# First layer of a two-block network: gated linear attention with values and gates projected 512 columns wide

## The chip, the cores and the metric

One core of one Trainium2 chip runs the whole program; the other cores are idle. The metric is the device time of one execution in microseconds (us). TensorE is called PE here, VectorE DVE, ScalarE ACT, GpSimd POOL and SyncE SP.

## What is computed

The network has a first block of four layers (gated linear attention, spatial gating, forgetting attention, gated linear attention) and a second block of two layers with a context stream. The sequence is 512 tokens of width 1024. The change touches the mixer of layer 0 alone. Cut to what matters:

```python
GLA_HEADS, GLA_DK, GLA_DV = 4, 128, 256

def gla_mixer(h, w_in, w_a2, b_a, g_head, w_out):
    q, k, v, z, a_low = jnp.split(h @ w_in, [512, 1024, 2048, 3072], axis=-1)
    log_a = jax.nn.log_sigmoid(a_low @ w_a2 + b_a) / 16.0
    q = q * 128 ** -0.5
    # per head, chunk by chunk, with a running sum b of log_a inside a chunk:
    #   o     = (q * exp(b)) @ state + (causal, decayed q k^T) @ v
    #   state = exp(b_last) * state + (k * exp(b_last - b))^T @ v
    o = rms_norm(o, g_head)                 # per head
    return (o * jax.nn.silu(z)) @ w_out
```

The mixer is called for layers 0 and 3 with other weights.

## The kernel before

Every projection is made in three products, so that it keeps the precision of 32 bits: each operand is split into a high and a low part (`split`, L256: ACT writes the high part at L258, DVE or POOL the low part at L259), and PE adds high times high, high times low and low times high in one PSUM bank. The hidden state H is kept transposed and split, 8 pieces of 128 channels.

`proj_tok` (L290) makes a projection with the tokens on the partitions: a piece of H for one tile of 128 tokens is the stationary operand, the weights are streamed (L312, L313, L314). At 256 columns it loads two channel pieces of weights at a time (256 KB) and puts two token tiles in one PSUM bank, so that four tiles take two banks; it has four steps. At more than 256 columns each token tile has a bank of its own, weights come one channel piece at a time (256 KB again), and the last two pieces form one step: seven steps. `proj_T` (L344) makes queries and keys transposed, 512 tokens wide (L360 to L362), in two banks. The banks of projections are a ring of four (`pp`), those of all else another ring of four (`pa`).

`gla` (L663) runs head by head. Short names for its steps, with the head as a number:

- V: 256 columns of values (`values`, L670), two copies by ACT into SBUF (L675)
- decay: gates of the decay for all heads (`gla_decay`, L702), once
- Q: queries and keys of the head (L684), evicted by ACT (L686) and DVE (L687)
- P: the decayed products of queries and keys (`gla_pairs`, L738). Seven levels; each has two subtractions and a multiplication on DVE (L754, L755, L759), an exponential on ACT (L756), a multiplication on POOL (L758), four small products on PE (L765) and a masked copy on DVE (L769)
- Z: 256 columns of gates (L693), each bank evicted by ACT (L632) and then DVE (L633), multiplied by the head gain on POOL (L698)
- Hd: the scan over four chunks (`gla_head`, L772), which ends with transposes (L820); `Odone` (L654) then splits the head's output

The order in the program is V0, decay, Q0, P0, Z0, Hd0, and for each later head Q, P, V, Z, Hd. The output projection `outproj` follows, in four blocks of 256 columns; a block's four weight pieces belong to one head each, so three quarters of a block can run before the last head is done.

The generators hand control back at each `yield`. `drain` (L458) then does 0.6 of a step of a background queue in layer 0: modulation matrices for later layers are loaded (512 KB a step) and multiplied (`mods`, L382, products at L395). The order of the instructions on an engine is made when the program is built: a scheduler with a model of times takes the instruction of highest priority (earliest in the program) that its model has ready. On the chip each engine then runs its list in order.

Of the kernel before, what the change touches and what calls it, by code (L numbers as in the profile page):

```python
# [15 lines left out]
AF = mybir.ActivationFunctionType  # L16
ALU = mybir.AluOpType
# [59 lines left out]
class Core:  # L77
# [585 lines left out]
    def gla(self, H, j, O):  # L663
        nc, A = self.nc, self.A
        W = A["gla_w_in"][j]
        gh = self.bcast(A["gla_g_head"][j].rearrange("h d -> (h d)"), 1024, "t4")
        nc.vector.tensor_scalar(gh, gh, 0.5, None, ALU.mult)
        b = []

        def values(h, v):  # L670
            o = []
            yield from self.proj_tok(H, 4, W, 8, 1024 + h * 256, 256, o, lead=LEAD[0] if h == 0 else 1)
            v.append(self.t("t4", [128, 4, 256]))
            for i in range(2):
                nc.scalar.copy(v[0][:, 2 * i:2 * i + 2], o[0][i])  # L675

        for h in range(4):
            v = []
            if h == 0:

                yield from values(h, v)
                yield from self.gla_decay(H, j, b)
            o = []
            yield from self.proj_T(H, 512, W, 8, [h * 128, 512 + h * 128], o)  # L684
            qT, kT = self.t("t2", [128, 512]), self.t("t2", [128, 512])
            nc.scalar.activation(qT, o[0][0], AF.Copy, scale=128 ** -0.5)  # L686
            nc.vector.tensor_copy(kT, o[0][1])  # L687
            at = []
            yield from self.phase("glah", self.gla_pairs(b[h], qT, kT, at))
            if h:  # L690
                yield from values(h, v)
            o = []
            yield from self.proj_tok(H, 4, W, 8, 2048 + h * 256, 256, o)  # L693
            zg = self.t("t4", [128, 4, 256])
            for i in range(2):
                self.silu2(zg[:, 2 * i:2 * i + 2], o[0][i])
            for t in range(4):
                nc.gpsimd.tensor_tensor(zg[:, t], zg[:, t], gh[:, h * 256:(h + 1) * 256], op=ALU.mult)  # L698
            yield from self.phase("glah", self.gla_head(h, b[h], qT, kT, v[0], zg, at[0], O))
            self.Odone(O, h)  # L700

    def gla_decay(self, H, j, b):  # L702
# [69 lines left out]
    def gla_head(self, h, b, qT, kT, v, zg, at, O):  # L772
        nc = self.nc
        v4 = lambda x: x.rearrange("p (c n) -> p c n", c=4)
        eq = self.t("t2", [128, 512])
        nc.scalar.activation(eq, b, AF.Exp, scale=1.0 / 16)
        dec = self.small("gdec", [128, 4])
        nc.vector.tensor_copy(dec, v4(eq)[:, :, 127])
        qd = self.t("t2", [128, 512])
        nc.gpsimd.tensor_tensor(qd, qT, eq, op=ALU.mult)  # L780
        ek = self.t("t2", [128, 512])
        nc.vector.tensor_tensor(v4(ek), v4(b)[:, :, 127:128].to_broadcast([128, 4, 128]), v4(b), op=ALU.subtract)
        nc.scalar.activation(ek, ek, AF.Exp, scale=1.0 / 16)
        nc.vector.tensor_tensor(ek, kT, ek, op=ALU.mult)
        ps = self.psA()
        for c in range(3):
            cs = slice(c * 128, (c + 1) * 128)
            nc.tensor.transpose(ps[:, cs], ek[:, cs], self.ident)
        kd = self.t("t2", [128, 384])
        nc.scalar.copy(kd, ps[:, :384])  # L790
        yield
        ops = []
        S = None
        pos = []
        for c in range(4):
            cs = slice(c * 128, (c + 1) * 128)
            po = self.psA()
            nc.tensor.matmul(po[:, :256], at[:, c], v[:, c], start=True, stop=(c == 0))
            if c:
                nc.tensor.matmul(po[:, :256], qd[:, cs], S, start=False, stop=True)  # L800
            if c < 3:
                ps = self.psA()
                nc.tensor.matmul(ps[:, :256], kd[:, cs], v[:, c], start=True, stop=True)
                S2 = self.t("t1", [128, 256])
                if S is None:
                    nc.vector.tensor_copy(S2, ps[:, :256])
                else:
                    nc.vector.scalar_tensor_tensor(S2, S, dec[:, c:c + 1], ps[:, :256], ALU.mult, ALU.add)
                S = S2
            sq = self.t("t1", [128, 256])  # L810
            ss = self.small("ss", [128, 1])
            nc.scalar.activation(sq, po[:, :256], AF.Square, accum_out=ss)
            r = self.rstd1(ss, 256)
            if c % 2 == 0:
                ops.append(self.t("t2", [128, 2, 256]))
            nc.vector.scalar_tensor_tensor(ops[c // 2][:, c % 2], po[:, :256], r, zg[:, c], ALU.mult, ALU.mult)
        for kk in range(2):
            ps = self.psA()
            for c in range(4):
                nc.tensor.transpose(ps[:, c * 128:(c + 1) * 128], ops[c // 2][:, c % 2, kk * 128:(kk + 1) * 128],  # L820
                                    self.ident)
            nc.scalar.copy(self.Opiece(O, h * 2 + kk), ps)
        yield
# [1449 lines left out]
LEAD = (1, 1, 1, 1, 2)  # L2273
# [66 lines left out]
```

## Time and profile before

| | |
|---|---|
| median of 3 runs | 3252.29 us (3252.24 to 3263.88) |
| profiled execution | 3250.65 us |
| its span, first to last instruction | 3248.6 us |
| PE busy | 3074.4 us, 95% of the span |
| DVE, ACT, POOL busy | 1733.8, 1461.0, 1318.9 us |
| mean granted PE clock | 0.975 of 2.4 GHz |

The profile names instructions by line, engine, operation and tiles: `gla.pp` is a PSUM bank of a projection in the mixer, `glah.pa` one of P or Hd, `mods.pa` one of the background products, `out.pp` one of the output projection. "Idle before, releaser" is the time for which the engine stood still ahead of an instruction, and what ended it. A matmul's own duration overlaps its neighbours; from one start to the next is what it costs in a stream.

### The profile page before, as it was taken

The page shows a single profiled execution, that of the slowest core. Times are in us where ns is not written, and L with a number is a line of the kernel's source. Part 1 is how long each engine was busy: PE and PEld are TensorE (multiplying, and loading weights), DVE is VectorE, ACT ScalarE, POOL GpSimd, SP SyncE. Part 2 cuts the span into 40 slices and gives each one's busy share as a digit, 9 for nine tenths or more (in the row PEclk, how much of TensorE's full clock was granted, in tenths as well). Part 3 has the DMA queues.
Part 4 walks back from the last instruction along what each step waited for, and adds up shares of the span by engine and source line. Part 5 has one row for each costly group of instructions (what it writes and reads, how often), then busy time and mean ns, then how long its engine had stood idle before and what let it go on. Part 6 is the DMA issues. An engine that isn't in the chain of part 4 may idle for free.

```text
span 3248.6 us, 60794 instructions
## 1 busy us (share of the span) xinstructions
PE 3074.4 (95%) x23263; PEld 2642.0 (81%) x23263; DVE 1733.8 (53%) x3586; ACT 1461.0 (45%) x3205; POOL 1318.9 (41%) x1314
## 2 busy tenths in 40 slices
PE   7999999999999999998989999899999989999999
PEld 4878889878877788887877889898888967888887
DVE  2744564454555465666888667541444468641212
ACT  3434544454544543455545544443324357643323
POOL 2544453232212345454542123554555441254445
PEclk8999999999989999999999999899999989999999
DMA  7355645754435624234664334443555330043332
GB/s 240 92 153 171 214 133 164 228 172 127 134 118 177 180 61 103 61 114 124 178 176 119 104 103 131 145 130 114 167 190 163 103 82 2 29 141 98 97 123 90
DMA packets 477386, 426.20 MB, mean 131 GB/s; under 512 B 108022, under 2 KB 421577, under 8 KB 477097
## 3 DMA queue, kind: packets, MB, share of 16 engines
q1 hardware_dynamic: 477097, 422.33, 43.4%
q8 instruction: 183, 3.00, 0.4%
q14 instruction: 106, 0.87, 0.1%
HBM read 383.66 MB, written 38.01 MB: 130 GB/s over the span
## 4 chain that ended last, share of the span: by engine, by line
PE 41%; DVE 5%; POOL 2%; ACT 1%; issue 1%; DMA 1%; SPq 0%; POOLq 0%; DVEq 0%; ACTq 0%
PE ffn.pp L360 6%; PE ffn.pp L361 6%; PE ffn.pp L362 5%; PE ffn.pa L314 2%; PE ffn.pa L312 2%; PE ffn.pa L313 2%; PE odda.pa L1122 1%; PE odda.pa L931 1%; PE mla.pp L1745 1%; PE out.pp L312 1%; PE out.pp L314 1%; PE out.pp L313 1%; PE mla.pa L1122 1%; PE gdng.pa L1593 1%; PE ffn.pp L313 1%
## 5 line engine op out<-in xcount | busy, mean ns | idle before, releaser
L259 POOL TENSOR_TENSOR ffn.wl<-ffn.wr,ffn.wh 128x512 fp32r<-128x512 f32 x258 | 341.3, 1326 | 340.2 <-ACT ffn.wh L258 340.0
L258 ACT ACTIVATE ffn.wh<-ffn.wr 128x512 fp32r<-128x512 f32 x258 | 162.5, 631 | 342.4 <-PE ffn.pp L362 128.9
L360 PE MATMUL ffn.pp<-pre.t,ffn.wh 128*128 128x512 f32 x672 | 261.8, 390 | 0.0
L361 PE MATMUL ffn.pp<-pre.t,ffn.wl 128*128 128x512 f32 x672 | 261.5, 389 | 0.0
L362 PE MATMUL ffn.pp<-pre.t,ffn.wh 128*128 128x512 f32 x672 | 261.5, 389 | 0.0
L312 PE MATMUL gla.pp<-gla.wh,pre.t 128*128 128x256 f32 x512 | 151.5, 296 | 0.6 <-ACT pre.t L258 0.6
L313 PE MATMUL gla.pp<-gla.wl,pre.t 128*128 128x256 f32 x512 | 150.1, 293 | 0.0
L314 PE MATMUL gla.pp<-gla.wh,pre.t 128*128 128x256 f32 x512 | 149.1, 292 | 0.5 <-DVE pre.t L259 0.5
L259 POOL TENSOR_TENSOR gla.wl<-gla.wr,gla.wh 128x512 fp32r<-128x512 f32 x66 | 88.2, 1337 | 150.0 <-ACT gla.wh L258 141.2
L259 POOL TENSOR_TENSOR ffn.cwl<-ffn.cwr,ffn.cwh 128x512 fp32r<-128x512 f32 x44 | 61.3, 1392 | 214.4 <-ACT ffn.cwh L258 172.0
L360 PEld LDWEIGHTS ffn.pp<-pre.t,ffn.wh 128*128 128x128 f32 x672 | 126.2, 188 | 26.7 <-issue 0.8
L362 PEld LDWEIGHTS ffn.pp<-pre.t,ffn.wh 128*128 128x128 f32 x672 | 126.2, 188 | 26.3
L361 PEld LDWEIGHTS ffn.pp<-pre.t,ffn.wl 128*128 128x128 f32 x672 | 126.2, 188 | 26.1
L633 DVE SCALAR_TENSOR_TENSOR ffn.t<-ffn.t,ffn.pp 128x512 f32<-128x512 f32 (+1 forms) x66 | 39.3, 595 | 196.3 <-ACT ffn.t L632 196.2
L258 ACT ACTIVATE ffn.cwh<-ffn.cwr 128x512 fp32r<-128x512 f32 x132 | 82.9, 632 | 104.8 <-PE ffn.pp L362 40.6
L312 PE MATMUL sgu.pp<-sgu.wh,pre.t 128*128 128x256 f32 x384 | 112.0, 292 | 6.9 <-DVE gdnp.at L1306 6.0
L313 PE MATMUL ffn.pa<-ffn.wl,ffn.t 128*128 128x512 f32 x304 | 118.3, 389 | 0.0
L314 PE MATMUL ffn.pa<-ffn.wh,ffn.t 128*128 128x512 f32 x304 | 118.3, 389 | 0.0
L1177 DVE SCALAR_TENSOR_TENSOR ffn.t<-ffn.t,ffn.pp 128x512 f32<-128x512 f32 (+1 forms) x66 | 39.4, 597 | 143.6 <-PE ffn.pp L362 143.0
L395 PE MATMUL mods.pa<-mods.wm,cond_c 128*32 128x256 f32 x1152 | 100.4, 400 | 14.8 <-DMA mods.wm<-in_w_mod_dram 14.5
L312 PE MATMUL ffn.pa<-ffn.wh,ffn.t 128*128 128x512 f32 x304 | 112.7, 389 | 0.0
L312 PE MATMUL fox.pp<-fox.wh,pre.t 128*128 128x256 f32 x384 | 110.9, 289 | 0.7 <-ACT fox.t L1002 0.5
(831 smaller groups left out, 10757.0 us busy)
## 6 DMA issues: line engine op xcount, KB each, us to landing
mods.wm<-in_w_mod_dram SPq DMA_DIRECT2D x176, 512.0 KB
gla.wr<-in_gla_w_in_dram SPq DMA_DIRECT2D x96, 256.0 KB
ffn.wr<-in_w_ffn_gate_dram SPq DMA_DIRECT2D x88, 256.0 KB
ffn.wr<-in_w_ffn_up_dram SPq DMA_DIRECT2D x88, 256.0 KB
ffn.wr<-in_w_ffn_down_dram SPq DMA_DIRECT2D x88, 256.0 KB
fox.wr<-in_fox_w_in_dram SPq DMA_DIRECT2D x64, 256.0 KB
sgu.wr<-in_sgu_w_in_dram SPq DMA_DIRECT2D x48, 256.0 KB
out.res_x<-out.t SPq DMA_DIRECT2D x24, 512.0 KB
```

What stands on the lines that cost most here:

```text
L258: nc.scalar.activation(hi, src, AF.Copy)
L259: (lo_eng or nc.vector).tensor_tensor(lo, src, hi.bitcast(F32), op=ALU.subtract)
L312: nc.tensor.matmul(o, H.hi(kk, s), w[0][:, k], start=(kk == 0 and first), stop=False)
L313: nc.tensor.matmul(o, H.hi(kk, s), w[1][:, k], start=False, stop=False)
L314: nc.tensor.matmul(o, H.lo(kk, s), w[0][:, k], start=False, stop=(kk == K - 1 and last))
L360: nc.tensor.matmul(o, wh[:, k], H.hi(kk), start=(kk == 0), stop=False)
L361: nc.tensor.matmul(o, wl[:, k], H.hi(kk), start=False, stop=False)
L362: nc.tensor.matmul(o, wh[:, k], H.lo(kk), start=False, stop=(kk == K - 1))
L395: nc.tensor.matmul(ps[g * 32:(g + 1) * 32, :256], pad[:, j, :], ws[j][:, g * 256:(g + 1) * 256], start=(j == 0), stop=(j == 7))
L633: nc.vector.scalar_tensor_tensor(dst, dst, 1.0, z, ALU.add, ALU.mult)
L1122: nc.tensor.matmul(po[e * 64:(e + 1) * 64, it * 128:(it + 1) * 128], v(e, j), PT[e][:, j * 128:(j + 1) * 128], start=(j == 0), stop=(j == ...
L1177: nc.vector.scalar_tensor_tensor(f, sg, 0.5, o[1], ALU.mult, ALU.mult)
```

## The change

In layer 0 the values of heads 0 and 1 are projected together, 512 columns wide, ahead of head 0, and those of heads 2 and 3 together between P and Hd of head 1. The gates of heads 0 and 1 are projected together between P and Hd of head 0; the gates of heads 2 and 3 keep their own 256-wide projection. The order becomes V01, decay, Q0, P0, Z01, Hd0, Q1, P1, V23, Hd1, Q2, P2, Z2, Hd2, Q3, P3, Z3, Hd3. Layer 3 (`j` is 1) keeps the order of before in a copy of the old code. `gla_head` takes lists of chunks in place of tiles.

```diff
+        if j:
+            ...  (the loop of before, for layer 3)
+            return
+        def pieces(x, e, w=256):
+            return [x[t // 2][:, t % 2, e * w:(e + 1) * w] for t in range(4)]
+
         def values(h, v):
+            x = [self.t("t4", [128, 2, 512]) for _ in range(2)]
             o = []
-            yield from self.proj_tok(H, 4, W, 8, 1024 + h * 256, 256, o, lead=LEAD[0] if h == 0 else 1)
-            v.append(self.t("t4", [128, 4, 256]))
-            for i in range(2):
-                nc.scalar.copy(v[0][:, 2 * i:2 * i + 2], o[0][i])
+            yield from self.proj_tok(H, 4, W, 8, 1024 + h * 256, 512, o, lead=LEAD[0] if h == 0 else 1,
+                                     each=lambda t: nc.scalar.copy(x[t // 2][:, t % 2], o[0][t]))
+            v += [pieces(x, e) for e in range(2)]
+
+        def gates(h, n, z):
+            x = [self.t("t4", [128, 2, n * 256]) for _ in range(2)] if n > 1 else [self.t("t4", [128, 4, 256])]
+            o = []
+            if n > 1:
+                def each(t):
+                    self.silu2(x[t // 2][:, t % 2], o[0][t])
+                    nc.gpsimd.tensor_tensor(x[t // 2][:, t % 2], x[t // 2][:, t % 2], gh[:, h * 256:(h + n) * 256], op=ALU.mult)
+                yield from self.proj_tok(H, 4, W, 8, 2048 + h * 256, 512, o, each=each)
+                z += [pieces(x, e) for e in range(n)]
+                return
+            ...  (256 columns as before)
+
+        v, z = [], []
         for h in range(4):
-            v = []
             if h == 0:
-                yield from values(h, v)
+                yield from values(0, v)
                 yield from self.gla_decay(H, j, b)
             ...  (queries, keys, pairs)
-            if h:
-                yield from values(h, v)
-            ...  (256 columns of gates)
-            yield from self.phase("glah", self.gla_head(h, b[h], qT, kT, v[0], zg, at[0], O))
+            if h == 0:
+                yield from gates(0, 2, z)
+            elif h == 1:
+                yield from values(2, v)
+            else:
+                yield from gates(h, 1, z)
+            yield from self.phase("glah", self.gla_head(h, b[h], qT, kT, v[h], z[h], at[0], O))
             self.Odone(O, h)
```

## Rows read from the trace of the kernel before

**Rows 1.** The page's head: span, then busy time and instructions of each engine.
```profile
span 3248.6 us, 60794 instructions
...
PE 3074.4 (95%) x23263; PEld 2642.0 (81%) x23263; DVE 1733.8 (53%) x3586; ACT 1461.0 (45%) x3205; POOL 1318.9 (41%) x1314
```
**Rows 2.** Stretches: length, busy time of five engines, PE clock, DMA share, GB/s.
```profile
36.00:88.00 52.00, 45.06 (x239) 32.98 (x241) 23.20 (x56) 24.71 (x46) 16.64 (x15) 0.86 0.59 166
88.00:300.00 212.00, 204.25 (x1532) 176.93 (x1525) 122.65 (x200) 78.35 (x150) 103.38 (x111) 1.00 0.41 123
```
**Rows 3.** The same view, by stage: P0, Hd0, P1, Hd1, P2, Hd2, P3, Hd3.
```profile
91.00:119.00 28.00, 26.46 (x196) 22.70 (x195) 25.66 (x42) 11.18 (x18) 17.74 (x17) 1.00 0.35 111
119.00:141.20 22.20, 22.20 (x157) 20.86 (x157) 8.14 (x18) 6.15 (x16) 8.18 (x12) 1.00 0.31 84
138.90:166.20 27.30, 26.11 (x200) 24.37 (x202) 23.27 (x37) 13.29 (x23) 17.66 (x15) 1.00 0.18 49
166.20:191.20 25.00, 24.68 (x181) 18.19 (x181) 7.04 (x12) 5.27 (x14) 10.67 (x15) 1.00 0.71 211
191.20:215.20 24.00, 21.26 (x173) 20.22 (x171) 19.62 (x31) 10.22 (x17) 13.56 (x11) 1.00 0.27 77
215.20:246.20 31.00, 31.00 (x209) 23.22 (x209) 9.72 (x19) 8.66 (x20) 12.20 (x17) 1.00 0.61 188
244.90:268.80 23.90, 21.94 (x181) 21.05 (x179) 19.38 (x31) 10.04 (x18) 14.37 (x12) 1.00 0.20 64
268.80:296.50 27.70, 27.70 (x228) 23.81 (x228) 10.15 (x19) 8.30 (x20) 8.82 (x15) 1.00 0.48 152
```
**Rows 4.** What PE waited for, 88 to 300 us: total, times, longest.
```profile
PE glah.pa L765 <- POOL glah.t L758: 6.7, 11, 1.3
```
**Rows 5.** Timeline of PE, an unbroken stream 256 columns wide: start, duration, instruction.
```profile
216.45 0.28 PE L313 MATMUL gla.pp<-gla.wl,pre.t 128*128 128x256 f32 x1
...
219.08 0.28 PE L314 MATMUL gla.pp<-gla.wh,pre.t 128*128 128x256 f32 x1
```
**Rows 6.** Timeline of PE, an unbroken stream 512 wide from the same lines.
```profile
2229.08 0.39 PE L312 MATMUL ffn.pa<-ffn.wh,ffn.t 128*128 128x512 f32 x1
...
2232.93 0.39 PE L314 MATMUL ffn.pa<-ffn.wh,ffn.t 128*128 128x512 f32 x1
```
**Rows 7.** Timeline of PE about the end of Z0 and of P0.
```profile
107.48 0.28 PE L314 MATMUL gla.pp<-gla.wh,pre.t 128*128 128x256 f32 x1
...
110.23 0.50 PE L360 MATMUL gla.pp<-pre.t,gla.wh 128*128 128x512 f32 x1
...
118.11 1.00 PE L765 MATMUL glah.pa<-glah.t 128*128 128x64 f32 x8
```
**Rows 8.** Timeline of DVE: the evictions of Z0's two banks.
```profile
109.11 0.68 DVE L633 SCALAR_TENSOR_TENSOR gla.t<-gla.t,gla.pp 128x512 f32<-128x512 f32 x1
...
112.81 0.67 DVE L633 SCALAR_TENSOR_TENSOR gla.t<-gla.t,gla.pp 128x512 f32<-128x512 f32 x1
```
**Rows 9.** Instructions that write the mixer's tiles on ACT: duration min/median/max.
```profile
L675 ACT COPY gla.t<-gla.pp x6: 566/578/589, 144.6 to 256.9; 128x512 f32<-128x512 f32 x6
```
**Rows 10.** The same on POOL, 88 to 300 us.
```profile
L698 POOL TENSOR_TENSOR gla.t<-gla.t,gla.t x16: 720/742/1255, 110.8 to 278.2; 128x256 f32<-128x256 f32 x16
L780 POOL TENSOR_TENSOR glah.t<-gla.t,glah.t x4: 1297/1450/1727, 116.9 to 267.4; 128x512 f32<-128x512 f32 x4
```
**Rows 11.** Groups by line and shape on PE, 88 to 300 us: busy, mean ns, idle before.
```profile
L765 PE MATMUL glah.pa<-glah.t 128*128 128x64 f32 x224 | 29.6, 276 | 7.4 <-POOL glah.t L758 6.7 <-DVE glah.t L759 0.5
...
L395 PE MATMUL mods.pa<-mods.wm,cond_c 128*32 128x256 f32 x208 | 17.8, 390 | 0.3 <-DMA mods.wm<-in_w_mod_dram 0.3
```
**Rows 12.** Output projection's matmuls that start before 296.3 us: count, durations, first and last start.
```profile
L312 PE MATMUL out.pp<-out.wh,gla.t x33: 278/283/472, 276.8 to 295.9; 128*128 128x256 f32 x33
L313 PE MATMUL out.pp<-out.wl,gla.t x32: 277/282/469, 277.1 to 295.1; 128*128 128x256 f32 x32
L314 PE MATMUL out.pp<-out.wh,gla.t x32: 278/282/469, 277.3 to 295.2; 128*128 128x256 f32 x32
```
**Rows 13.** What PE waited for, 300 to 420 us.
```profile
PE mods.pa L395 <- DMA mods.wm<-in_w_mod_dram: 2.1, 2, 1.6
```

More of the change, by code (lines that the diff above doesn't have):

```diff
@@ L668, in gla, with values @@
         b = []
+        if j:
+            def values(h, v):
+                o = []
+                yield from self.proj_tok(H, 4, W, 8, 1024 + h * 256, 256, o, lead=LEAD[0] if h == 0 else 1)
+                v.append(self.t("t4", [128, 4, 256]))
+                for i in range(2):
+                    nc.scalar.copy(v[0][:, 2 * i:2 * i + 2], o[0][i])
+            for h in range(4):
+                v = []
+                if h == 0:
+                    yield from values(h, v)
+                    yield from self.gla_decay(H, j, b)
+                o = []
+                yield from self.proj_T(H, 512, W, 8, [h * 128, 512 + h * 128], o)
+                qT, kT = self.t("t2", [128, 512]), self.t("t2", [128, 512])
+                nc.scalar.activation(qT, o[0][0], AF.Copy, scale=128 ** -0.5)
+                nc.vector.tensor_copy(kT, o[0][1])
+                at = []
+                yield from self.phase("glah", self.gla_pairs(b[h], qT, kT, at))
+                if h:
+                    yield from values(h, v)
+                o = []
+                yield from self.proj_tok(H, 4, W, 8, 2048 + h * 256, 256, o)
+                zg = self.t("t4", [128, 4, 256])
+                for i in range(2):
+                    self.silu2(zg[:, 2 * i:2 * i + 2], o[0][i])
+                for t in range(4):
+                    nc.gpsimd.tensor_tensor(zg[:, t], zg[:, t], gh[:, h * 256:(h + 1) * 256], op=ALU.mult)
+                yield from self.phase("glah", self.gla_head(h, b[h], qT, kT, [v[0][:, c] for c in range(4)], [zg[:, c] for c in range(4)], at[0], O))
+                self.Odone(O, h)
+            return
@@ new lines, in gates @@
+        def gates(h, n, z):
+            x = [self.t("t4", [128, 2, n * 256]) for _ in range(2)] if n > 1 else [self.t("t4", [128, 4, 256])]
+            o = []
+            if n > 1:
[5 more added lines that the diff above has]
+                return
+            yield from self.proj_tok(H, 4, W, 8, 2048 + h * 256, 256, o)
+            for i in range(2):
+                self.silu2(x[0][:, 2 * i:2 * i + 2], o[0][i])
+            for t in range(4):
+                nc.gpsimd.tensor_tensor(x[0][:, t], x[0][:, t], gh[:, h * 256:(h + 1) * 256], op=ALU.mult)
+            z.append([x[0][:, t] for t in range(4)])
@@ L689, in gla @@
             yield from self.phase("glah", self.gla_pairs(b[h], qT, kT, at))
-            if h:
-                yield from values(h, v)
-            o = []
-            yield from self.proj_tok(H, 4, W, 8, 2048 + h * 256, 256, o)
-            zg = self.t("t4", [128, 4, 256])
-            for i in range(2):
-                self.silu2(zg[:, 2 * i:2 * i + 2], o[0][i])
-            for t in range(4):
-                nc.gpsimd.tensor_tensor(zg[:, t], zg[:, t], gh[:, h * 256:(h + 1) * 256], op=ALU.mult)
-            yield from self.phase("glah", self.gla_head(h, b[h], qT, kT, v[0], zg, at[0], O))
+            if h == 0:
+                yield from gates(0, 2, z)
[4 more added lines that the diff above has]
+            yield from self.phase("glah", self.gla_head(h, b[h], qT, kT, v[h], z[h], at[0], O))
             self.Odone(O, h)
@@ L797, in gla_head @@
             po = self.psA()
-            nc.tensor.matmul(po[:, :256], at[:, c], v[:, c], start=True, stop=(c == 0))
+            nc.tensor.matmul(po[:, :256], at[:, c], v[c], start=True, stop=(c == 0))
             if c:
@@ L802, in gla_head @@
                 ps = self.psA()
-                nc.tensor.matmul(ps[:, :256], kd[:, cs], v[:, c], start=True, stop=True)
+                nc.tensor.matmul(ps[:, :256], kd[:, cs], v[c], start=True, stop=True)
                 S2 = self.t("t1", [128, 256])
@@ L815, in gla_head @@
                 ops.append(self.t("t2", [128, 2, 256]))
-            nc.vector.scalar_tensor_tensor(ops[c // 2][:, c % 2], po[:, :256], r, zg[:, c], ALU.mult, ALU.mult)
+            nc.vector.scalar_tensor_tensor(ops[c // 2][:, c % 2], po[:, :256], r, zg[c], ALU.mult, ALU.mult)
         for kk in range(2):
```

## Prediction

> **What bounds the kernel now.** I began with the page's head: PE is busy for 95% of the span [rows 1]. The chain of work that ended last doesn't reach back to this mixer, so I went to the stretches. The mixer of layer 0 fills 36 to 300 us. In the first 52 us PE is busy for 45.06 at a mean granted clock of 0.86; in the next 212 us it is busy for 204.25 at full clock, and no other engine comes near (DVE 122.65) [rows 2]. So a microsecond of matmuls taken out of the second stretch should come off the time, if PE doesn't idle instead.
>
> The stages show where it could idle [rows 3]. A P stage is DVE's: 25.66 of 28.0, 23.27 of 27.3, 19.62 of 24.0 and 19.38 of 23.9 us busy. PE fills it with projections and stands still for 1.54, 1.19, 2.74 and 1.96 us, 7.4 in all; in the four Hd stages it idles for 0.3. The wait list names the cause: the small products of P wait for POOL, 6.7 us in 11 waits [rows 4]. P2 and P3 idle most although each had a V and a Z, 192 matmuls, to run beside it, P0 less with only a Z of its own. The idle time is therefore not a lack of work but the fixed order: a small product stands in PE's list where the model had its operands ready, and they come later.
>
> **The change part by part.** *Matmuls.* Values and gates of four heads were 8 projections of 96 matmuls, 256 wide: 768. Now there are 3 of 96 at 512 wide and 2 of 96 at 256: 576 narrow ones give way to 288 wide ones. In a stream a narrow one costs (219.08 - 216.45) / 22 = 0.1195 us [rows 5], a wide one of the same form, stationary tokens and streamed weights, (2232.93 - 2229.08) / 17 = 0.2265 [rows 6]. A pair saves 0.239 - 0.2265 = 0.0126 us, and 288 pairs save 3.6 us. One of the three wide projections lies where the mean clock is 0.86; if none of its 96 saved anything, 1.2 us less. I take 3.6.
>
> The Trainium skill ("TensorE: Matmul & The Clock Gate", section "Back-to-back issue gap") gives the gap of a matmul of N columns at full clock as N/2.4 + 2.5 ns: 109.2 and 215.8 ns. By that a pair saves 2.5 ns and the change 0.7 us. Rows 5 and 6 are both longer, by 10 ns each, so the trace has a larger fixed cost for each matmul and the saving goes by the trace.
>
> *Loads and splits.* A step of either width loads 256 KB: 8 x 4 = 32 loads before, 3 x 8 + 2 x 4 = 32 after, with as many splits on ACT, DVE and POOL. A step lasts 24 x 0.1195 = 2.87 or 12 x 0.2265 = 2.72 us on PE. V1's loads move ahead on SP's queue to a stretch with a DMA share of 0.59 [rows 2]; they ask for the same rate as V0's, and only for longer. Nothing is put in front of the loads of the constants, which still go out after the first step. Cost: nothing.
>
> *Evictions.* ACT makes 8 copies of 128x512 for values as before, ACT and DVE 8 each for gates. POOL made 16 multiplications of 0.742 us (median), and now makes 8 of these and 4 at twice the width, 1.45 us for that size [rows 10]: 11.7 in place of 11.9. POOL is half idle.
>
> *Banks.* A wide projection holds all four banks of the projection ring. Before, Q1 could start at 110.23 in the two banks that Z0 left free, while Z0, over at 107.6, gave up its banks at 109.8 and 113.5 [rows 7, 8]: its DVE evictions stood in line behind P0's work. Now Q1 must wait for the bank of Z01's first token tile. Queued behind that wait on PE are the rest of P0 and Hd0. The last step of a wide projection does two channel pieces, 6 matmuls for a tile, so the first tile is ready 18 x 0.2265 = 4.1 us before the last. If DVE serves it as fast as Z0's first bank (2.2 us after), PE waits for nothing; if as late as Z0's second, 5.9 us. I take 1.0, nearer to the first bank, since it is the first that is wanted. Behind V01 and V23 the evictions are ACT's alone, 0.58 us each [rows 9], well within 4.1; behind V01 there is the decay's work too. Nothing for these.
>
> The Trainium skill ("Perfetto Trace Analysis", section "Matmuls") says that independent matmul groups should rotate through different PSUM banks, so that the evacuation of one overlaps the matmuls of the next; it also says that larger matmuls are the more efficient. The first speaks against the change, the second for it. Rows 7 and 8 show such an overlap, which the change gives up at one place.
>
> *Order.* V1 moves ahead of the decay, Z1 beside P0. P0 and P1 have 96 wide matmuls beside them, 21.7 us; P2 and P3 have 96 narrow ones, 11.5 us, in place of 23. P0 had just that before, and pulled Q1 forward from 110.23, before its last level at 118.11 [rows 7], at an idle time of 1.54. For P2 there is Q3, for P3 the output projection. So I put nothing on the idle time of the P stages, with bounds from the 4.7 us of P2 and P3 saved to 10.0 us lost (below).
>
> *Background.* The mixer's yields fall from 61 to 58. At 0.6 a yield, 1.8 steps of 8 small products and 512 KB each move from layer 0 to layer 1; 8 products were 8/208 of 17.8 us, 0.7 us [rows 11]. The sum of work is the same. The first need for them in layer 0's output projection takes 33 steps (three parts of 11), and 0.6 x 59 = 35 are done by the mixer's end, so no burst is forced. PE waited 2.1 us for such loads between 300 and 420 us [rows 13]: bounds of 2.1 either way, value nothing.
>
> The sum, against the profiled execution: 3250.65 - 3.6 + 1.0 = 3248.05. The median of the runs is 1.64 above that execution, which gives 3249.7 for the median. Alone, this forecast spreads over 3246 to 3253 by the banks and the background.
>
> **The rivals.**
>
> *A: the chain of heads is rigid.* P and Hd alternate from 91.0 to 296.5 us, because all share the other four banks in program order. V01 makes P0 start 96 x (0.2265 - 0.1195) = 10.3 us later. If the chain keeps its length, the end of Hd3 moves by 10.3; PE fills part with the output projection: two of its blocks without the last head's quarter are 144 matmuls, 97 of which already ran by then [rows 12], so 47 x 0.1195 = 5.6 us. That is 10.3 - 5.6 = 4.7 us slower, 3257.0. It decides if the eight stages can't shorten by 8.3 us (10.3 + 3.6 - 5.6). Against it: with the shortest P and Hd of rows 3 four heads take 4 x (23.9 + 22.2) = 184.4 us, 21 less than now.
>
> *B: thin cover, slower than before.* If nothing is pulled forward into P2 and P3, a P of 23.9 us has its own small products, 29.6 / 4 = 7.4 [rows 11], and 11.5 of gates beside it: 5.0 us idle, 10.0 for both. -3.6 + 10.0 = 6.4 us slower, 3258.7. It decides from the point where P outlasts the 18.9 us. Against it stands P0 as it was.
>
> *C: the bank.* The full 5.9 us at Q1: -3.6 + 5.9, so 3254.6.
>
> *D: better fill.* P2 and P3 lose the 4.7 us that they idle: -3.6 - 4.7, so 3244.0. The order is made anew and could suit the chip better; nothing in the trace says that it will.
>
> *E: no saving.* The 3.6 us don't appear since PE idles for as long elsewhere, or the wide form here costs two narrow ones: 3252.3.
>
> **How the numbers follow.** Forecast 0.46, A 0.16, B 0.14, C 0.08, D 0.12, E 0.04. The likeliest gives 3249.7. The range runs from D with the background's 2.1 off, 3242, to B with 2.1 on, 3261. Half a per cent, about what a measurement of this kernel can tell from no change, is 16.3 us: below 3236.0 nothing leads but D with the early stalls gone as well, 0.03; above 3268.6 A, B and C must each pay in full (-3.6 + 8.3 + 10.0 + 5.9 = 20.6), 0.05. The rest, 0.92, is no change.
>
> **What would show it.** In the changed trace: 288 wide matmuls of `gla.pp` in layer 0 at 0.2265 us apart; P0 some 10 us later; Q3 between the levels of P2, output projection between those of P3 (against B); no idle time ahead of Q1's first matmul beyond 1 us (against C); Hd3 over at about 297 us or before, with more than 97 output matmuls behind it (against A); idle time of the P stages near 7.4 us. The prediction is wrong if P2 and P3 idle for over 5 us each, or if the order after 300 us changes by more than the moved background steps.

## The result and the profile after

The change costs half a per cent: 3273.14 us, the median of seven runs (3268.7 to 3275.58), beside 3252.29 us for the kernel before in the same comparison (3247.84 to 3263.88). The ratio is 1.0058, with a 95% interval of 1.0047 to 1.0069, that is 19 us (15 to 22). The forecast was 3249.7 us, "no change", within 3242 to 3261, so time, range and sign were all wrong. The profiled execution of the changed kernel took 3273.14 us, that of the kernel before 3250.65; these two are compared below.

The page's head of the changed kernel answers to rows 1:

```profile
span 3271.3 us, 60217 instructions
...
PE 3079.3 (94%) x22975; PEld 2630.5 (80%) x22975; DVE 1725.5 (53%) x3586; ACT 1463.0 (45%) x3207; POOL 1314.8 (40%) x1310
```

PE has 288 matmuls fewer and yet 4.9 us more of busy time; the span is 22.7 us longer, so 17.8 us are idle time. The next fence, stretches of the changed kernel (start:end, length, busy us of PE, PEld, DVE, ACT and POOL, PE clock, DMA share, GB/s), says where. The first eight are P0, Hd0, P1, Hd1, P2, Hd2, P3, Hd3; a P stage runs on to Hd's first product here, while in rows 3 it ends with its last small product, which in P2 and P3 of the kernel before is 4.0 and 6.7 us sooner. Then come layer 0's output projection, the start of layer 1 up to its last transposes, layer 1's mixer, and layer 1's output projection.

```profile
100.50:129.00 28.50, 27.67 (x160) 22.16 (x159) 24.03 (x44) 13.02 (x22) 16.52 (x14) 1.00 0.30 83
128.00:159.00 31.00, 31.00 (x165) 22.00 (x164) 8.04 (x14) 9.10 (x22) 14.43 (x18) 1.00 0.50 153
158.00:184.50 26.50, 24.88 (x154) 19.62 (x154) 21.28 (x35) 12.28 (x21) 14.98 (x13) 1.00 0.40 114
183.80:205.70 21.90, 21.90 (x131) 18.49 (x130) 5.76 (x11) 7.13 (x18) 8.09 (x12) 1.00 0.35 90
205.60:237.00 31.40, 28.48 (x192) 23.26 (x189) 24.76 (x36) 11.39 (x19) 18.55 (x17) 0.89 0.40 132
236.70:258.50 21.80, 21.80 (x153) 18.89 (x152) 6.24 (x12) 6.07 (x16) 6.25 (x11) 1.00 0.35 110
257.20:289.20 32.00, 27.58 (x203) 26.80 (x202) 24.92 (x39) 12.01 (x20) 17.42 (x15) 0.89 0.14 44
289.00:303.80 14.80, 12.78 (x83) 9.44 (x81) 6.37 (x11) 5.64 (x16) 5.83 (x10) 0.88 0.39 126
303.80:343.80 40.00, 36.85 (x314) 32.31 (x314) 13.08 (x33) 16.94 (x51) 13.51 (x19) 0.96 0.69 237
343.80:380.30 36.50, 28.84 (x227) 23.08 (x226) 21.48 (x51) 23.14 (x58) 18.49 (x28) 0.86 0.81 267
380.30:589.40 209.10, 201.08 (x1713) 186.13 (x1712) 106.50 (x197) 92.87 (x171) 92.17 (x77) 0.98 0.51 148
589.40:665.00 75.60, 68.52 (x572) 60.40 (x570) 30.19 (x70) 24.73 (x62) 15.66 (x17) 0.95 0.72 223
```

The same three later places in the kernel before, which the prediction had not looked at by stage: layer 0's output projection, start of layer 1, layer 1's output projection.

```profile
296.50:338.80 42.30, 41.80 (x362) 37.20 (x360) 18.74 (x39) 22.15 (x63) 17.77 (x23) 1.00 0.80 268
338.80:368.40 29.60, 25.74 (x222) 21.43 (x221) 22.45 (x49) 21.33 (x52) 17.51 (x27) 1.00 0.85 276
576.10:642.50 66.40, 64.61 (x564) 58.03 (x562) 29.65 (x69) 25.17 (x63) 15.65 (x17) 1.00 0.76 244
```

Three places make up most of the loss in this pair of executions. Layer 0 is over 5.0 us later (343.7 in place of 338.7): the eight stages begin 9.5 us later and get only 2 us shorter. The start of layer 1 lasts 36.5 us in place of 29.6, 6.9 more, with PE idle for 7.7 in place of 3.9 and the granted clock at 0.86 in place of 1.00. Layer 1's output projection lasts 75.6 us in place of 66.4, 9.2 more; the mixer between the two adds 1.4. The table sets milestones of PE against the kernel before. By the end of layer 1 22.6 us are lost, and at the end of the span 22.7: nothing net is won or lost behind layer 1.

| us later than before, at the end of | Hd3 | layer 0 | start of layer 1 | mixer of layer 1 | layer 1 | layer 2's mixer | layer 3 | last FFN |
|---|---|---|---|---|---|---|---|---|
| before, at | 296.2 | 338.7 | 368.3 | 576.1 | 642.4 | 1014.0 | 1516.1 | 3240.4 |
| changed kernel | 7.2 | 5.0 | 11.8 | 13.3 | 22.6 | 19.1 | 16.9 | 22.7 |
| e1 (yields back) | 4.4 | 2.5 | 1.8 | 2.9 | 5.1 | 8.9 | 6.6 | 12.4 |
| e2 (before, fewer steps) | -0.8 | -4.2 | 2.9 | 3.6 | 11.8 | 11.8 | 13.8 | 16.6 |
| e3 (order, narrow) | 14.9 | 14.2 | 14.6 | 15.4 | 15.6 | 15.0 | 18.0 | 20.0 |
| e4 (before, more steps) | 0.5 | 0.6 | -0.4 | -1.1 | 0.6 | 5.8 | 2.9 | 5.1 |
| e5 (Z01 alone) | 3.5 | 5.3 | 7.1 | 7.4 | 7.5 | 17.1 | 18.7 | 21.4 |
| e6 (V23 alone) | 7.4 | 7.4 | 5.6 | 6.4 | 6.6 | 7.4 | 11.3 | 16.5 |
| e9 (V01 alone) | -1.3 | -1.2 | -1.3 | -1.4 | -1.4 | 4.4 | 6.1 | 8.7 |
| e10 (steps repaid) | 2.6 | 1.7 | 6.9 | 8.7 | 10.4 | 11.3 | 12.4 | 17.7 |
| e11 (before, spread) | 2.1 | 2.4 | 2.7 | 3.7 | 3.9 | -0.8 | 1.0 | 3.3 |
| e12 (e1, spread) | 4.4 | 2.3 | 2.5 | 4.9 | 5.4 | 3.1 | 4.6 | 8.7 |

Each row is one execution, and executions of one kernel differ: 21 of the kernel before ran from 3243.0 to 3265.1 us. So verdicts on whole times go by the ratios below, and the table serves to find places. The executions of e1, e5 and e7 (below) lie 6.0, 7.5 and 9.3 us above the medians of their kernels, that of e4 4.9 below. How well a place repeats can be read from programs that have the same lists of instructions up to there: e10 has those of the changed kernel until it is in layer 1's mixer, and e11 those of the kernel before through layer 0. At the end of layer 0 e10 stands at 1.7 where the changed kernel stands at 5.0, and e11 at 2.4 where the kernel before stands at 0. So layer 0's loss of 5.0 us is known to some 3 us only. The start of layer 1 repeats better (6.9 and 5.2 us; 0 and 0.3); behind layer 1 differences of 5 to 10 us come and go.

The theory I went to the chip with: most of the loss is the 1.8 background steps that three missing yields move out of layer 0, the smaller part is layer 0's order. The rivals: the order alone does it; or any new order costs this much, whichever steps it moves.

### The profile page after: what moved, and what is told of

Its sections match the earlier page's. It is cut to its first block, busy times and chain, and to the rows that moved or that the text cites. A ratio compares the mean times of both kernels' runs of the same rounds, so it can differ in the third digit from the quotient of the medians.

```text
span 3271.3 us, 60217 instructions
## 1 busy us (share of the span) xinstructions
PE 3079.3 (94%) x22975; PEld 2630.5 (80%) x22975; DVE 1725.5 (53%) x3586; ACT 1463.0 (45%) x3207; POOL 1314.8 (40%) x1310
## 4 chain that ended last, share of the span: by engine, by line
PE 71%; DVE 11%; DMA 5%; ACT 4%; POOL 3%; issue 3%; SPq 1%; DVEq 0%; POOLq 0%; ACTq 0%
PE ffn.pp L360 5%; PE ffn.pp L361 5%; PE ffn.pp L362 5%; PE out.pp L312 3%; PE out.pp L314 2%; PE out.pp L313 2%; PE mods.pa L395 2%; PE ffn.pa L314 2%; PE ffn.pa L313 2%; PE ffn.pa L312 2%; DMA mods.wm<-in_w_mod_dram 2%; PE fox.pp L312 1%; PE fox.pp L314 1%; PE fox.pp L313 1%; PE gla.pp L312 1%
## 5 line engine op out<-in xcount | busy, mean ns | idle before, releaser
L312 PE MATMUL gla.pp<-gla.wh,pre.t 128*128 128x256 f32 (+1 forms) x416 | 132.1, 321 | 0.2 <-ACT pre.t L258 0.2
L313 PE MATMUL gla.pp<-gla.wl,pre.t 128*128 128x256 f32 (+1 forms) x416 | 131.8, 318 | 0.0
L314 PE MATMUL gla.pp<-gla.wh,pre.t 128*128 128x256 f32 (+1 forms) x416 | 131.1, 317 | 0.0
L258 ACT ACTIVATE gla.wh<-gla.wr 128x512 fp32r<-128x512 f32 (+1 forms) x98 | 60.8, 621 | 115.3 <-PE gla.pp L362 35.5
```

Source lines behind the costliest of these rows:

```text
L258: nc.scalar.activation(hi, src, AF.Copy)
L312: nc.tensor.matmul(o, H.hi(kk, s), w[0][:, k], start=(kk == 0 and first), stop=False)
L313: nc.tensor.matmul(o, H.hi(kk, s), w[1][:, k], start=False, stop=False)
L314: nc.tensor.matmul(o, H.lo(kk, s), w[0][:, k], start=False, stop=(kk == K - 1 and last))
```

## The experiments

**The yields.** e1 is the changed kernel with three yields given back; e2 is the kernel before with as many steps taken away and nothing else; e4 has the second diff with += in place of -=.

```diff
             self.Odone(O, h)
+            if h:
+                yield
```

```diff
             self.Odone(O, h)
+            if h and j == 0:
+                self.owed["m"] -= MRATE
```

> The changed kernel with one more yield after each of heads 1 to 3 of layer 0, so that the mixer has 61 yields again and the background queue gets 36.6 + 0.6 steps by its end, as before. Theory 1 (the shift of the background steps costs the time after layer 0): the 5 us by the end of layer 0's output projection stay, the 17 us that follow go, about 3257. Theory 2 (the other order of the heads' work costs it, wherever it shows): the time stays within 5 us of the changed kernel's 3273.

Measured for e1: 3257.17 us (10 runs), ratio 1.0022 [1.0011, 1.0034], the time that theory 1 had named. Three bare yields take the loss from 0.58% to 0.22%.

> The kernel before with 0.6 of a background step taken off after each of heads 1 to 3 of layer 0: 1.8 steps fewer by the mixer's end, as in the changed kernel, and nothing else. Theory 1 (background shift): 12 to 20 us slower than before, 3264 to 3272, all of it after 339 us. Theory 2 (order of the heads' work): the same as before within 5 us.

Measured for e2: 3266.91 us (4 runs), ratio 1.0050 [1.0033, 1.0067]. With every projection and its order left as they were, 1.8 steps fewer cost nearly as much as the whole change, as theory 1 had it. The table puts its loss in the same two places: 7.1 us at the start of layer 1 (2.9 + 4.2) and 8.2 in layer 1's output projection; layer 0 ends 4.2 earlier (it has less to do), and 4.8 more are lost behind layer 1. e1 and e2 together (0.22 + 0.50) exceed the change's 0.58, within their intervals.

> The kernel before with 0.6 of a background step added after each of heads 1 to 3 of layer 0: 1.8 steps more by the mixer's end. Theory 1 (background shift, fewer steps early cost): not slower than before, down to 10 us faster. Theory 2: the same within 5 us. A third reading, that any shift of these steps stirs the order of all that follows by some us either way, sees a change of 5 us or more of any sign.

Measured for e4: 3260.59 us (10 runs), ratio 1.0027 [1.0017, 1.0036]. The two places stay as before (0.6 us at the end of layer 1), and 5 us are lost in layer 2's mixer. Theory 1 had said not slower. So a third reading has something in it: moving steps in either direction makes the whole order anew, and that alone can cost 5 us somewhere. Part of e2's 0.50% may be of this kind too.

**Where the steps are missed.** Layer 1's output projection needs layer 2's modulation complete. What isn't done by then is forced: counted in the programs' order, 6 steps in the kernel before, in e1, e3, e5, e6, e9 and e10, 5 in e4, and 8 in the changed kernel and in e2. The loss of 8 to 9 us in this stage is there in the two kernels of the table that force 8, and in no other. PE's waits there in the changed kernel (stretch of layer 1's output projection: total, times, longest):

```profile
PE mods.pa L395 <- DMA mods.wm<-in_w_mod_dram: 4.1, 1, 4.1
PE out.pp L312 <- DVE out.t L596: 1.8, 1, 1.8
PE out.pa L476 <- DVE out.mra L474: 1.2, 1, 1.2
```

In the kernel before, the wait for these loads is 1.3 us in the same stage. e10 pays the 1.8 steps back in layer 1's mixer, late enough to leave the start of layer 1 as it is:

```diff
             self.Odone(O, c)
+            if c < 3:
+                self.owed["m"] += MRATE
             yield
```

> The changed kernel as it is in layer 0, with 0.6 of a background step added in each of three column groups of layer 1, so that the 1.8 missing steps are made up before layer 1's output projection. There the program forces what is still missing for layer 2's modulation: 6 steps in the kernel before, 8 in the changed one, 6 here. Theory 1a (the forced burst costs the 9 us of layer 1's output projection): that stretch is as long as before within 3 us, and the time about 3264; the 7 us at the start of layer 1 stay. If the burst is not the cause: about 3273.

Measured: 3269.53 us (4 runs), ratio 1.0046 [1.0031, 1.0061], where the theory had said about 3264. The place behaves as the theory has it, the total hardly: layer 1's output projection is 1.7 us over before in place of 9.3, the start of layer 1 keeps a loss of 5.2, but 5.3 us more are lost after layer 3. The stretches of e10 in that order (layer 0's output projection, start of layer 1, layer 1's output projection):

```profile
298.80:340.40 41.60, 38.26 (x319) 33.22 (x316) 13.02 (x33) 16.92 (x51) 13.46 (x19) 0.92 0.68 229
340.40:375.30 34.90, 27.64 (x227) 22.14 (x226) 21.33 (x51) 23.20 (x58) 18.51 (x29) 0.90 0.83 280
584.80:652.90 68.10, 64.69 (x564) 58.06 (x562) 29.70 (x69) 25.16 (x63) 15.67 (x17) 1.00 0.77 242
```

The start of layer 1 follows the same count: it is 5.2 to 7.1 us longer in the three kernels that come to it with 1.8 steps fewer (the changed one, e2, e10), and between -1.8 and +1.8 in all others of the table. PE's waits in that stretch of the changed kernel:

```profile
PE mods.pa L395 <- DMA mods.wm<-in_w_mod_dram: 4.3, 4, 2.2
PE .pa L476 <- DVE .mra L474: 3.4, 1, 3.4
```

Before, the stretch has one such wait for the loads, 1.6 us, and none for L474. e2 has both again, 4.0 and 4.0. What comes late is a modulation of the second block (`mod_b`): the context stream takes it up at the start of layer 1, where L474 sums it and L476 transposes it. In the programs' order it needs 55 steps; 58 are done by then in the kernel before and in e1, 56 in the changed kernel and in e2, so that nothing is forced. On the chip the last part of it is stored (L401) 5.7 us after the end of layer 0 in the kernel before and 2.3 after it in e1, but 19.9 and 18.4 after it in the changed kernel and in e2. SP's stores, in this order:

```profile
344.42 1.03 SPq L401 DMA_DIRECT2D mod_b<-mods.t  x2
343.47 1.03 SPq L401 DMA_DIRECT2D mod_b<-mods.t  x2
363.58 1.04 SPq L401 DMA_DIRECT2D mod_b<-mods.t  x2
352.88 1.03 SPq L401 DMA_DIRECT2D mod_b<-mods.t  x2
```

e1 has the changed kernel's order of heads and e2 that of the kernel before, so the late store goes with the steps and not with the order. How late the loads are asked for is to be read from SP's queue, where they stand in program order among the output projection's and the next mixer's. First the changed kernel, then the kernel before (start, time from the first issue of the group to the end of its last, line, transfer, count):

```profile
244.76 0.34 SPq L391 DMA_DIRECT2D mods.wm<-in_w_mod_dram  x1
...
263.82 32.74 SPq L281 DMA_DIRECT2D out.wr<-in_gla_w_out_dram  x9
298.82 2.17 SPq L281 DMA_DIRECT2D sgu.wr<-in_sgu_w_in_dram  x3
302.80 1.70 SPq L391 DMA_DIRECT2D mods.wm<-in_w_mod_dram  x2
```

```profile
256.46 15.99 SPq L281 DMA_DIRECT2D out.wr<-in_gla_w_out_dram  x5
272.65 0.35 SPq L391 DMA_DIRECT2D mods.wm<-in_w_mod_dram  x1
...
296.08 0.34 SPq L391 DMA_DIRECT2D mods.wm<-in_w_mod_dram  x1
```

In the changed kernel SP sends no modulation weights for 58 us (244.76 to 302.80): nine loads of the output projection, pulled forward to fill P3, stand in front. They wait in part for buffers that DVE's weight splits set free, as the list of SP's waits tells (changed kernel, 240 to 310 us):

```profile
SPq L281 <- DVE out.wl L259: 16.1, 4, 4.7
```

The DMA engines are nearly empty meanwhile (0.14 busy, 44 GB/s, in the seventh stretch above). The kernel before sends six in the stretch shown, from 272.65 on, one by one between the others. That the queue makes the loads late in the changed kernel is read from the trace; no run changed the queue's order alone, and other runs speak against giving it much weight. e1 sends no such load for 47 us (236.15 to 282.91), and its start of layer 1 loses nothing; e2 has a pause of 29 us (245.96 to 275.19), no longer than the kernel before (242.13 to 272.65), and has both waits.

**Without the loads.** e7 (the kernel before) and e8 (the changed one) leave the modulation weights' loads out and multiply a constant in their place.

```diff
-                ws.append(self.wp.tile([128, D], F32, name=self.nm("wm"), tag="wm", bufs=WM))
-                nc.sync.dma_start(ws[k], W[k * 128:(k + 1) * 128, v * D:(v + 1) * D])
+                ws.append(None)
...
-                                     ...  ws[j][:, g * 256:(g + 1) * 256]
+                                     ...  self.ident[:, None, :].to_broadcast([128, 2, 128])
```

> The kernel before, with the background products of L395 reading the identity matrix in place of loaded weights: the products, yields and evictions stay, the 512 KB load of every step is left out, so the modulation is not the reference's. It is the base for the next run. All theories: faster than before by some of the 14.5 us that PE waited for such loads, 3225 to 3250.

> The changed kernel with the same loads left out. Theory 1 (the loss is that of background loads that come late, behind the output projection's loads on SP, and then collide at the start of layer 1): the difference to the run before it is small, -4 to +6 us. Theory 2 (the order of the heads' work costs the time with or without those loads): the difference stays at 15 us or more.

Measured: e7 3233.63 us (4 runs), 0.9951 [0.9934, 0.9969]; e8 3244.21 us (10 runs), 0.9971 [0.9960, 0.9982]. Without the loads the change costs 0.20% by the ratios (10.6 us by the medians) in place of 0.58%, between what the two theories had said; with four runs of e7 the 0.20% are not clear of nothing. By the milestones e8 ends layer 0 7.9 us behind e7, its start of layer 1 is 3.8 us shorter than e7's, its mixer of layer 1 7.2 longer and its output projection of layer 1 1.2 longer: the losses of 6.9 and 9.2 us need the loads, and layer 0's does not. What lengthens the mixer is not known.

**Layer 0, part by part.** e3 makes the order of the change with narrow projections (V0 V1 first, Z0 Z1 beside P0, V2 V3 beside P1); e5, e6 and e9 make one projection wide each and leave the rest. All four have 61 yields; in the diffs of the last three, which are against the changed kernel, `values1` is the values' projection of one head, 256 wide.

e3, on the kernel before:

```diff
                 yield from values(h, v)
+                if first:
+                    ...
+                    yield from values(1, v)
...
-            if h:
-                yield from values(h, v)
-            ...
+            if first:
+                if h == 0:
+                    yield from gates(0, zs)
+                    yield from gates(1, zs)
+                elif h == 1:
+                    for i in (2, 3):
+                        ...
+                        yield from values(i, v)
+                else:
+                    yield from gates(h, zs)
```

> The order of the changed kernel in layer 0, but every projection 256 wide: V0 V1 ahead of the decay, Z0 Z1 beside P0, V2 V3 beside P1, Z2 beside P2, Z3 beside P3. 61 yields. If the order costs the time and the width saves 3.6 us: layer 0 some 8 us longer. Theory 1 (background shift) then sees nothing more, about 3261; theory 2 (order) sees the rest too, 3270 to 3280. If the width with its four banks is what costs: near 3252.

Measured for e3: 3267.56 us (4 runs), ratio 1.0054 [1.0037, 1.0071], between the two theories' times; layer 0 ends 14.2 us later, where 8 had been said. Against e1, which has the same order, the width is worth 11.7 us in layer 0 (10.4 by the medians of the whole), three times the 3.6 of the stream; why so much is not known.

```diff
-                yield from values(0, v)
+                yield from values1(0, v)
...
+            if h:
+                yield from values1(h, v)
             if h == 0:
                 yield from gates(0, 2, z)
-            elif h == 1:
-                yield from values(2, v)
-            else:
+            elif h > 1:
                 yield from gates(h, 1, z)
```

> The kernel before with only the gates of heads 0 and 1 made 512 wide beside P0 in layer 0, all values and the other gates 256 wide and at their old places; one more yield at the end, so 61. The background keeps its place, so theory 1 expects 3252 within 5 us, with layer 0 over within 2 us of before (1.2 us saved in matmuls, up to 3 lost to the order). If a wide projection by itself costs (four banks held, DVE evictions beside P0): layer 0 later by 4 us or more.

Measured for e5: 3264.39 us (10 runs), ratio 1.0028 [1.0011, 1.0045]; layer 0 ends 5.3 us later, so both forecasts of theory 1 missed. Its P0 with Z0 and Z1 behind it:

```profile
90.00:125.20 35.20, 32.58 (x162) 26.13 (x163) 24.47 (x45) 12.21 (x20) 16.45 (x14) 0.85 0.33 98
```

35.2 us to Hd's first product in place of 28, with 2.6 us idle and the clock at 0.85.

```diff
-                yield from values(0, v)
+                yield from values1(0, v)
...
+            if h == 1:
+                yield from values1(1, v)
+            elif h == 2:
                 yield from values(2, v)
...
+            yield from gates(h, 1, z)
```

> The kernel before with only the values of heads 2 and 3 made 512 wide, beside P2 in layer 0 and with Z2 behind them; V0, V1 and all gates 256 wide as before; one more yield at the end, so 61. P2 has 33 us of projections beside it and P3 only 11.5. Thin cover of P3 as the cause of the 5 us in layer 0: P3 lasts 30 us or more in place of 23.9 and layer 0 is over 3 to 6 us later. If a late P3 in the changed kernel was the wait of DVE for a modulation load instead: P3 stays near 24 to 28 us, layer 0 within 2 us.

Measured for e6: 3263.02 us (6 runs), ratio 1.0034 [1.0015, 1.0053]; layer 0 ends 7.4 us later. Its P2 with V23 and Z2:

```profile
190.70:230.50 39.80, 38.18 (x256) 32.48 (x255) 23.65 (x36) 16.13 (x28) 22.73 (x18) 0.91 0.44 132
```

Its P3, on which the expectation turned, lasts 28.0 us (254.2 to 282.2): too short for thin cover as the cause, while layer 0 is later than the other reading allows.

```diff
-            if h == 0:
-                ...
+            if h > 1:
+                yield from values1(h, v)
+            yield from gates(h, 1, z)
```

> The kernel before with only the values of heads 0 and 1 made 512 wide, ahead of the decay; V2 V3 and all gates 256 wide at their old places, one more yield at the end, so 61 and 6 forced steps. P1 has only Z1, 11.5 us, beside it. If the chain of P and Hd sets the length of layer 0, P0 starts 10 us later, P1 and Hd1 shorten by the V1 that left them, and layer 0 is over 0 to 5 us later; if PE sets it, 1.2 us earlier.

Measured for e9: 3257.68 us (10 runs), ratio 1.0010 [0.9998, 1.0021]; layer 0 ends 1.2 us earlier. V01 is the one wide projection that lies ahead of the chain of P and Hd and not between them. The 1.2 us have the size of what its stream saves, 96 x 0.0126 = 1.2, but they are less than what two executions of one list differ by at this place, and the whole can't be told from the kernel before. One between P and Hd brings a second head's work into the stage; the stage then outlasts the 28 us that P0 and P2 take to Hd's first product by 7.2 us in e5 and 11.8 in e6. That this is what makes layer 0 longer there is argued, not shown: e3 puts the same work in the same places 256 wide and is later still.

**A way out?** e11 and e12 spread the background so that nothing is forced in layer 1: a rate of 0.72 during its mixer, on the kernel before and on e1.

```diff
+                self.rate["m"] = 0.72
                 yield from self.phase("sgu", self.sgu(H, O))
+                self.rate["m"] = MRATE
```

> The kernel before with a background rate of 0.72 in place of 0.6 in layer 1's mixer, so that no step is forced in its output projection (6 before). Theory 1a: the stretch between the end of layer 1's mixer and the start of layer 2's gets shorter by some 5 us, the whole down to 3245 if nothing else is stirred; a reading in which any shift of these steps costs: slower than before.

> The changed kernel with the three yields put back (as e1) and a background rate of 0.72 in layer 1's mixer, no step forced in its output projection. Theory 1a with the order's cost of 2 to 5 us in layer 0: 3247 to 3255. If it is under the kernel before it is a version that uses the wide projections with gain.

Measured: e11 3252.75 us (10 runs), 0.9992 [0.9981, 1.0003]; e12 3258.16 us (10 runs), 1.0010 [0.9997, 1.0022]; both are slower than was hoped. Forced steps are 0 in both. What PE waits for about layer 1's output projection (576 to 672 us), two rows of e11 and two of the kernel before:

```profile
PE pre.pa L536 <- DVE pre.t L565: 6.0, 2, 3.1
PE mods.pa L395 <- DMA mods.wm<-in_w_mod_dram: 1.6, 2, 0.8
```

```profile
PE mods.pa L395 <- DMA mods.wm<-in_w_mod_dram: 7.6, 5, 3.1
...
PE pre.pa L536 <- DVE mods.t L399: 0.5, 1, 0.5
```

So 6.0 us of waiting for loads are gone, and 5.5 have come at L536, behind DVE's normalisation for layer 2: one wait took the other's place. No version beat the kernel before; e9, e11 and e12 can't be told from it.

## Why the prediction was wrong, point by point

**Background: the step that failed.** It read "no burst is forced ... bounds of 2.1 either way, value nothing". Layer 0's need was worked out and is right: nothing is forced there. But a moved step passes every later need, and two later ones were never looked up: the second block's modulation at the start of layer 1, which had 3 steps to spare and then 1, and layer 2's in layer 1's output projection, which was 6 steps behind already and became 8. The bound came from PE's waits for loads between 300 and 420 us in the kernel before [rows 13], that is from how well the loads arrive when they are asked for in time; the cost of asking later is no row of that list. By the table the moved steps cost 6.9 + 9.3 us in the two places; e2, which does nothing but move them, gives 16.3 us (0.50%) for the whole, and the prediction had 0 ± 2.1.

**Order: nothing on P2 and P3.** Up to Hd's first product P2 and P3 last some 31 and 32 us in place of 28.0 and 30.6. First the kernel before, cut in this way, then e10, whose lists here are those of the changed kernel:

```profile
191.20:219.20 28.00, 25.26 (x214) 23.62 (x213) 22.86 (x35) 11.98 (x20) 14.85 (x12) 1.00 0.31 88
244.90:275.50 30.60, 28.64 (x238) 27.20 (x237) 23.21 (x37) 12.42 (x22) 15.74 (x13) 1.00 0.23 72
```

```profile
203.40:234.80 31.40, 27.92 (x188) 22.64 (x187) 24.74 (x36) 11.28 (x19) 18.49 (x16) 0.89 0.42 130
255.30:282.80 27.50, 24.51 (x201) 23.51 (x200) 23.80 (x38) 11.77 (x20) 17.36 (x15) 1.00 0.16 50
```

P2 is 3 us longer in both executions, P3 1 us longer in the one and 3 shorter in the other; e11, with the lists of the kernel before, has 30.0 and 31.4 us. So neither stage is clearly longer. PE idles for 2.9 and 4.4 us in the changed kernel, before for 2.7 and 2.0, which is within the bounds that the prediction set for the P stages. Q3 and the output projection did come in as cover, as was said; what was not seen is that cover can bring work to the engine that bounds P. DVE is busy for 24.8 and 24.9 us, before for 22.9 and 23.2. In P3 the splits of the output projection's weights are part of it: 3.4 us for four splits, before 2.1 for three. In P2 the splits take less than before, and what made DVE busier there was not found. In P3 it also stands still in program order. Groups of DVE in the seventh stretch (busy, mean ns, idle before and its releaser):

```profile
L259 DVE TENSOR_TENSOR out.wl<-out.wr,out.wh 128x512 fp32r<-128x512 f32 x4 | 3.4, 859 | 0.4 <-ACT out.wh L258 0.4
...
L474 DVE TENSOR_TENSOR out.mra<-out.mra,out.mrb 16x128 f32<-16x128 f32 x1 | 2.1, 2067 | 5.0 <-DMA out.mra<-mod_a 5.0
```

The sum of the next layer's modulation waits 5.0 us for a transfer, and P3's first DVE work (L805, at 263.29) is queued behind it though P3's products ran from 257.2. In the kernel before the same instruction waits 0.2 us, at 247.6; in e10 it waits 2.7.

**Rival A, the rigid chain,** gave 4.7 us for layer 0, and 5.0 came in the profiled execution, 1.7 in e10's; that the first is so near is partly luck, and A's three terms are only partly what happened. P0 began 9.5 us later (forecast 10.3). The chain shrank by 2.2 us, 205.5 to 203.3 (200.9 in e10), where 0 was said and 8.3 needed. All 144 output-projection matmuls that were to be had ran before the end of Hd3 (97 before [rows 12]), worth 5.6 us as worked out, and then PE idled: 2.0 us in Hd3. But the output projection got only 2.3 us shorter, since PE waits 3.1 us there for modulation weights (0.5 before) at a clock of 0.96. Without the loads it does get shorter, by 4.4 us (e8 is 12.3 us behind e7 at Hd3's end, 7.9 after the projection). A deserved more than 0.16; against it I had put the shortest P and Hd of four heads, which no order here has together.

**Rival B, thin cover:** not borne out. The idle time of P2 and P3 grew by 0.2 and 2.4 us, and not to 5.0 us of missing matmuls each.

**Rival C and the bank term of 1.0:** refuted. PE's groups by shape, 96 to 304 us of the changed kernel, give Q's products and the wide projections no idle time, and Q1's first matmul comes 1.57 us after Z01's last, with other products between them:

```profile
L312 PE MATMUL gla.pp<-gla.wh,pre.t 128*128 128x512 f32 x64 | 25.9, 407 | 0.0
...
L360 PE MATMUL gla.pp<-pre.t,gla.wh 128*128 128x512 f32 x48 | 20.3, 424 | 0.0
```

```profile
127.96 0.39 PE L314 MATMUL gla.pp<-gla.wh,pre.t 128*128 128x512 f32 x1
...
129.53 0.58 PE L360 MATMUL gla.pp<-pre.t,gla.wh 128*128 128x512 f32 x1
```

The loss that the rule on rotating banks would give (the Trainium skill, "Perfetto Trace Analysis", section "Matmuls") shows in no row here.

**Matmuls: the spacing is right.** An unbroken wide stream steps at (109.88 - 105.56) / 19 = 0.227 us, 0.2265 forecast:

```profile
105.56 0.39 PE L314 MATMUL gla.pp<-gla.wh,pre.t 128*128 128x512 f32 x1
...
109.88 0.39 PE L312 MATMUL gla.pp<-gla.wh,pre.t 128*128 128x512 f32 x1
```

That the 3.6 us came off the time is not shown: PE's busy time rose, and e9's 1.2 us lie within the scatter of single executions. By the gap that the Trainium skill states for an isolated matmul ("TensorE: Matmul & The Clock Gate", section "Back-to-back issue gap"), a condition that the prediction left out, the 96 pairs of one wide projection would save an estimated 96 x 2.5 ns = 0.2 us and not 1.2; the trace's own spacing decides.

**Range and chances.** The range was built of what layer 0 could do, and layer 0 alone (5.0 us) lies within it. The sentence on what would make the prediction wrong named the case, an order after 300 us that changes by more than the moved steps, and gave it no price; "slower by over 0.5%" had 0.05.

**What stays open.** Behind layer 1 every version of the table but the changed kernel and e11 loses 3 to 14 us in the profiles, e5 most of it in layer 2's mixer (9.6), and only e2 among them forces more steps than before. Part may be the scatter of single executions; what moves the rest wasn't found. Nor was it settled how much of the two places' loss is the lower clock (0.86 and 0.95 against 1.00) and how much the waiting beside it, nor why 8 forced steps cost some 8 us in layer 1's output projection and 6 no more than 0 do in e11.

## To carry to other kernels

Work that is paid out per yield, per loop turn or per head has due times far behind the code that is edited: when an edit changes the number of turns, list every later need of that work and what it is behind at each, and price the difference there. Cover pulled into a stage can cost on the engine that bounds the stage, here weight splits and an in-order wait on DVE in P3, so count its side work before calling it free. And two projections joined into one move the second one's work into an earlier stage: look at what that stage then holds beyond what bounds it, and don't count on the stream's saving alone.

## What was not expected of the hardware

An issue queue can hold transfers back while the DMA engines idle: SP held nine issues over 32.74 us, with the DMA share at 0.14 and the modulation weights' loads behind them. What that cost here is not shown. The granted clock is no plain function of PE's idle time: P2, P3 and the start of layer 1 had 0.89, 0.89 and 0.86 with 2.9, 4.4 and 7.7 us idle, a part of each at 1.2 GHz in place of 2.4, and before 1.00 each with 2.7, 2.0 and 3.9; e11, with the lists of the kernel before, had 0.89 in P2 with 2.4. And executions of one single-core kernel spread over 22 us (3243.0 to 3265.1 in 21 runs), more than this change costs, so that two single executions can't tell a difference of half a per cent.
